# Handing out side work after every column chunk of the input projection instead of after every quarter

## Chip, cores, metric

One core of a Trainium2 chip. The metric is device microseconds of one execution; the median of three runs of the kernel before is 2044.25 us (2044.1, 2044.25 and 2047.47 us).

## What is computed

One step of a hybrid decoder layer for 1024 prompt tokens and 8 decode tokens (1032 columns of activations, 2048 wide). The parts that matter here:

```
h = rmsnorm(x, norm_w)
p = h @ w_in                      # one wide projection, 7768 columns, split into q, k, v, indexer q/k, gates, ...
att  = dsa_prompt(...)            # per 128 queries: indexer scores, top 256 keys, softmax over those keys
h_ml = mlstm_run(...)             # chunked linear attention with a state that is carried along the sequence
...                               # the same two for 8 decode tokens, from paged caches and stored states
x = x + concat([att * silu(z_att), norm(h_ml) * sigmoid(o) * silu(z_ml)]) @ w_out
y = rmsnorm(x, final_norm_w)
```

Everything is float32 in and out. The matrix products run in a reduced float32 format, and each is made of three passes: operands are split into a high and a low part, and high x high, high x low and low x high are added up in PSUM.

## The kernel before

**The projection.** `w_in` is cut into 61 tiles of 128 columns (tile 0 has 88), named by `t`; their order is that of the constants `T_MISC` to `T_AZ`. For one tile, `proj` (L1359) runs four quarters `q`. A quarter covers four of the sixteen 128-row blocks of the contraction. Its weights come by one DMA on SyncE's queue (`wraw`, L210), are cast by ScalarE (`wH`, L213), and the rest is taken by VectorE (`wL`, L214). Then `mm` (L1351 to L1357) multiplies: for each of the three column chunks `c` of 344 activations (two chunks of 388 in tiles 1 to 8), 4 blocks x 3 passes = 12 matmuls into the PSUM tile `pj` of that chunk. So a quarter is 36 matmuls on TensorE, all on line L1356. After the fourth quarter `evac` (L319) takes the three `pj` tiles out on VectorE (`ev`, L333, or L331 where a scale is applied), and sends them on by DMA; for some tiles ScalarE applies sigmoid (L380, L385, L399).

**Side work.** Attention, recurrence and the decode tokens are written as Python generators ("jobs") that issue some instructions and then `yield` the weight of what is to come. Two `Lane`s hold them in order. Lane 0: `gates`, `index` (scores L458 to L463, the search for the 256th largest score L493 to L515, the mask L526 to L535), `att` (L538 on: scores L602, transposes L644, casts `ptH`, `ptL` L648 and L649, values L653), `ml` (recurrence, L775 on: transposes and products L817 to L822, casts L787 and L829, main products L841 to L847, `tail` L877). Lane 1: `dscore` (L964), `dsel` (L1000, L1080), `datt` (decode attention: L919 to L921, `qb` loads L1216, products L1235 and L1239, values L1280), `dml` (decode recurrence: loads `bc` L1149 and `Cb` L1152, scale L1163, update L1165).

Each job has a start and an end, counted in projection tiles. `Lane.step(now)` takes 1 off the lane's debt and then runs generator steps until the debt is paid; a step costs

```
quarters = max(1.0, self.job.end * 4 - self.now)
cost = w * quarters / max(self.left, w)
```

so that the job's remaining weight is spread over the remaining quarters. `proj` calls it once behind the three chunks of each quarter:

```
for lane in lanes:
    lane.step(ts[0] * 4 + q)
```

Jobs start at tile 9 (`T_AK`) at the earliest and the last ones are to end at tile 58 (`T_PRE`). At two places the rest of a job is run at once (`ensure`): `att` ahead of tile 53, `ml` and `dml` at tile 58.

**What sets the real order.** The Python order gives priorities. A list scheduler at build time reorders the instructions of every engine from these, from the data they need and from its own plan of how long each takes; `tc.high_priority()` lifts the loads and casts of projection weights and `evac`, and `pin` keeps single instructions in program order. Each engine then runs its list in order. Side products use five PSUM banks (`bank`), the projection three (`pj`).

**Behind the projection** come two output stages: L1483 (the part of the tokens from 640 on) and L1521 (tokens 0 to 639), which no lane takes part in.

Of the kernel before, what the change touches and what calls it, by code (L numbers as in the profile page):

```python
# [41 lines left out]
T_AK = 9  # L42
# [48 lines left out]
    return c  # L91


class Job:
    def __init__(self, name, start, end, weight, gen, *conds):
        self.name, self.start, self.end, self.weight, self.gen, self.conds = name, start, end, weight, gen, conds


class Lane:
# [7 lines left out]
    def _next(self):  # L107
        if self.cur is None:
            self.job = self.jobs.pop(0)
            self.left = self.job.weight  # L110
            self.cur = self.job.gen()
        try:
            w = next(self.cur)
        except StopIteration:
            self.done.add(self.job.name)
            self.cur = None
            return 0.0
        quarters = max(1.0, self.job.end * 4 - self.now)
        cost = w * quarters / max(self.left, w)
        self.left -= w  # L120
        return cost

    def _ready(self):
        return bool(self.jobs) and self.jobs[0].start * 4 <= self.now and all(f() for f in self.jobs[0].conds)

    def step(self, now):
        self.now = now
# [13 lines left out]
def body(tc, A, stop=None):  # L141
# [58 lines left out]
    def bank(n=512, dt=F32, parts=128):  # L200
        t = psg.tile([128, 512], F32, name="bank")
        return t
# [15 lines left out]
    def wsplit(src, cols, pool, raws, bufs, tie=False, tag=""):  # L218
        H, L, load, cast = wload(src, cols, pool, raws, bufs, tag)
        dma = load(slice(0, 4))  # L220
        if tie:
            pin(dma)
        cast(slice(0, 4))
        return H, L
# [81 lines left out]
    def chunks(t):  # L306
        return CHQ if T_IQ <= t < T_AK else CH
# [1015 lines left out]
    def mixload(ci, k, pool, tie=False):  # L1323
        c0, cn = CB[ci]
        h = pool.tile([128, cn], F32R, name=f"mH{k}", bufs=1)
        l = pool.tile([128, cn], F32R, name=f"mL{k}", bufs=1)
        dma = SY.dma_start(l.bitcast(F32), gateV[k, :, c0:c0 + cn])
        if tie:
            pin(dma)
        src = attS[k // 4][(k % 4) * 128:(k % 4 + 1) * 128] if k < 8 else hS[(k - 8) * 128:(k - 7) * 128]  # L1330
        SY.dma_start(h.bitcast(F32), src[:, c0:c0 + cn])
        return ci, k, pool, h, l

    def mixmake(ci, k, pool, h, l, tie=False, tmp=None):
        c0, cn = CB[ci]
        oo, mr = h.bitcast(F32), l.bitcast(F32)
        mx = (tmp or pool).tile([128, cn], F32, name="mx", bufs=2)
        if k < 8:
            v = V.tensor_tensor(mx, mr, oo, OP.mult)
        else:  # L1340
            v = V.scalar_tensor_tensor(mx, oo, mlw[:, k - 8:k - 7], mr, OP.mult, OP.mult)
        if tie:
            pin(v)
        SC.copy(h, mx)
        V.tensor_tensor(l, mx, h.bitcast(F32), OP.subtract)
        mixb[ci][k] = (h, l)

    def wsrc(t, q):
        return A["wm"][q] if t == 0 else A["wa"][t - 1, q]

    def mm(ps, cols, t, q, c, H, L):  # L1351
        c0, cn = chunks(t)[c]
        for k in range(4):
            kk = q * 4 + k
            for w_, x_, z in ((H, xH, 0), (H, xL, 1), (L, xH, 2)):
                PE.matmul(ps[:cols, :cn], w_[:, k, :cols], x_[kk][:, c0:c0 + cn],  # L1356
                          start=(kk == 0 and z == 0), stop=(kk == 15 and z == 2))  # L1357

    def proj(ts, hook=None):  # L1359
        pss = []  # L1360
        for x, t in enumerate(ts):
            nc_ = len(chunks(t))
            if x:
                pss.append([bank() for c in range(nc_)])
            else:
                pss.append([psj.tile([128, 512], F32, name=f"pj{(t * nc_ + c) % 3}") for c in range(nc_)])
        for q in range(4):
            ws = []
            for x, t in enumerate(ts):
                cols = NMISC if t == 0 else 128  # L1370
                with tc.high_priority():
                    if hook and x == 0:
                        hook(q, ws)
                    elif hook and not q:
                        pass
                    elif x:
                        ws.append(wsplit(wsrc(t, q), cols, x0, 2, 4, q == 1))
                    else:
                        ws.append(wsplit(wsrc(t, q), cols, wst, 2, 3))
            for x, t in enumerate(ts):  # L1380
                cols = NMISC if t == 0 else 128
                H, L = ws[x]
                for c in range(len(pss[x])):
                    mm(pss[x][c], cols, t, q, c, H, L)
            for lane in lanes:
                lane.step(ts[0] * 4 + q)
            if len(mids) > 3 or mids and not pend:
                for _ in range(2):
                    mixmake(*mids.pop(0), True)
            for k in pend[:2]:  # L1390
                mids.append(mixload(0, pend.pop(0), pb0, True))
        return pss
# [4 lines left out]
    def xhook(q, ws):  # L1397
# [4 lines left out]
        for k in range(max(1, q * 4), q * 4 + 4):  # L1402
            xload(k)
            if k == 2:
                SY.dma_start(cst, A["cst"][:, :NCST])
                with tc.tile_pool(name="c0", bufs=1) as c0p:
# [3 lines left out]
                    V.tensor_copy(cmask[:, 128:256], ctmp[:, 128:256])  # L1410

    pss = proj((0, 1, 2), xhook)
    with tc.high_priority():
        for _ in row_rstd([acc], rstd, R, x0):
            pass
    x0ctx.close()
    with tc.tile_pool(name="mp", bufs=1) as mp, tc.tile_pool(name="iqp", bufs=1) as iqp:
        with tc.high_priority():
            misc = evac(0, pss[0], NMISC, mp)
        with tc.high_priority():  # L1420
            for t in (1, 2):
                evac(t, pss[t], 128, iqp)
        for t in range(3, T_AK):
            pss = proj((t,))
            with tc.high_priority():
                evac(t, pss[0], 128, iqp)
            if t == 3:
                index_weights(misc)
    for t in range(T_AK, NT):
        if t == T_AZ:  # L1430
            lanes[0].ensure("att")
        norms = load_norms(t) if t >= T_AZ else None
        pss = proj((t,))
        if t == T_PRE:
            lanes[0].ensure("ml")
            lanes[1].ensure("dml")
            pb0 = mctx.enter_context(tc.tile_pool(name="pb0", bufs=1, side="right"))
        with tc.high_priority():
            evac(t, pss[0], 128, None, norms)
        if t == T_PRE:  # L1440
            pend += PRE
# [67 lines left out]
    def resid(g):  # L1509
        for b in range(NBK):  # L1510
            yt[b][g] = pt.tile([128, 512], F32, name=f"yt{b}{g}")
            SY.dma_start(yt[b][g], A["x2"][b, :, g * 512:g * 512 + 512])
        f = pt.tile([128, 512], F32, name="fnr")
        SY.dma_start(f, A["fnr"][g * 512:g * 512 + 512].partition_broadcast(128))
        return f
# [34 lines left out]
    for g in range(4):  # L1550
        ps = [bank() if x is None else psj.tile([128, 512], F32, name=f"pj{x}") for x in homes[g]]
        ws = []
        for n in range(KT):
# [5 lines left out]
            if n == 5:  # L1559
                f = resid(g)  # L1560
# [94 lines left out]
```

## Time and profile before

| | |
|---|---|
| median of three runs | 2044.25 us |
| profiled execution | 2045.44 us, of which 2043.7 us are its span |
| outside the span | 1.74 us |
| TensorE (PE) busy | 2027.0 us, 99% of the span |
| VectorE (DVE), ScalarE (ACT), GpSimd (POOL) busy | 58%, 40%, 11% |
| mean granted TensorE clock | 0.997 |

Times are microseconds from the first instruction. PE's matmuls overlap in the records (each is shown for 0.32 us where a new one starts every 0.157 us), so a busy time counts stretches in which some matmul was under way.

### The profile page before, as it was taken

To read this page: it belongs to the slowest core of one execution; us is meant where nothing else is said; L and a number is where in the kernel's file an instruction comes from. 1 tells how busy PE (TensorE), PEld (TensorE's weight loads), DVE (VectorE), ACT (ScalarE), POOL (GpSimd) and SP (SyncE) were. 2 spreads that over 40 slices of the span, in tenths; PEclk is the share of its full clock that TensorE was granted. 3 is DMA by queue.
4 is the path that set the end of the run, shared out by engine and by line. 5 is a ranking of instruction groups with operands and counts; after the bars stand their busy time and mean duration, and the time that the engine had idled before them with its cause. 6 is when DMAs were issued, how large, how long until landed. Compare 5 with 4: busy or idle time off the path is not lost.

```text
span 2043.7 us, 34345 instructions
## 1 busy us (share of the span) xinstructions
PE 2027.0 (99%) x12678; PEld 1954.4 (96%) x12678; DVE 1178.0 (58%) x2955; ACT 820.5 (40%) x1616; POOL 233.7 (11%) x294
## 2 busy tenths in 40 slices
PE   9999999999999999999999999999999999999998
PEld 8999999999999999999999999999999999998886
DVE  8333357656686776878354554446677456664331
ACT  8121234233531455312256666544454334433221
POOL 0000111100000000023110011012222211101110
PEclk9999999999999999999999999999999999999999
DMA  7444533322222212244322332146675558566212
GB/s 246 105 112 125 155 109 114 102 81 65 79 70 75 77 49 67 68 140 155 112 74 82 111 96 85 48 130 197 210 216 174 149 183 315 176 224 223 81 49 103
DMA packets 203669, 257.08 MB, mean 126 GB/s; under 512 B 39685, under 2 KB 130885, under 8 KB 203501
## 3 DMA queue, kind: packets, MB, share of 16 engines
q1 hardware_dynamic: 198253, 240.82, 37.9%
q0 software_dynamic: 4096, 12.59, 2.0%
q8 instruction: 99, 1.62, 0.3%
q10 hardware_dynamic: 1152, 1.49, 0.2%
q14 instruction: 69, 0.57, 0.1%
HBM read 195.00 MB, written 59.82 MB: 125 GB/s over the span
## 4 chain that ended last, share of the span: by engine, by line
PE 94%; issue 2%; DVE 2%; ACT 1%; DMA 1%; SPq 0%; POOLq 0%; POOL 0%; DVEq 0%; ACTq 0%
PE pj L1356 61%; PE bank L1483 7%; PE bank L1521 6%; PE pj L1521 4%; PE bank L458 3%; PE bank L653 2%; PE bank L602 2%; PE bank L644 1%; PE bank L964 1%; PE bank L1356 1%; DMA xr<-in_xT_dram 1%; PE bank L841 1%; PE bank L847 1%; PE bank L843 1%; PE bank L1080 0%
## 5 line engine op out<-in xcount | busy, mean ns | idle before, releaser
L1356 PE MATMUL pj<-xH,wH 128*128 128x344 f32 (+2 forms) x2736 | 882.9, 324 | 3.0 <-DVE ev L333 1.5
L1356 PE MATMUL pj<-xH,wL 128*128 128x344 f32 (+2 forms) x2736 | 882.2, 323 | 0.0
L1356 PE MATMUL pj<-xL,wH 128*128 128x344 f32 (+2 forms) x2736 | 881.9, 323 | 0.0
L1356 PEld LDWEIGHTS pj<-xH,wH 128*128 128x128 f32 (+1 forms) x2736 | 513.8, 188 | 6.4 <-ACT wH L213 1.8
L1356 PEld LDWEIGHTS pj<-xL,wH 128*128 128x128 f32 (+1 forms) x2736 | 513.6, 188 | 2.9 <-DVE xL L266 0.9
L1356 PEld LDWEIGHTS pj<-xH,wL 128*128 128x128 f32 (+1 forms) x2736 | 514.1, 188 | 2.2
L213 ACT CAST wH<-wraw 128x512 fp32r<-128x512 f32 (+2 forms) x375 | 228.8, 614 | 642.4 <-PE pj L1356 413.0
L214 DVE TENSOR_TENSOR wL<-wraw,wH 128x512 fp32r<-128x512 f32 (+2 forms) x375 | 263.5, 708 | 339.7 <-ACT wH L213 325.3
L507 ACT ACTIVATE eq<-eq 128x512 bf16<-128x512 bf16 (+2 forms) x93 | 78.4, 843 | 114.1 <-DVE eq L506 111.4
L333 DVE TENSOR_TENSOR ev<-pj,rstd 128x344 f32<-128x344 f32 x144 | 74.0, 514 | 70.3 <-PE pj L1356 58.1
L460 ACT ACTIVATE rl<-bank 128x512 f32<-128x512 f32 (+2 forms) x160 | 78.7, 522 | 89.0 <-PE bank L458 63.3
L463 DVE SCALAR_TENSOR_TENSOR s<-rl,wiN,s 128x512 f32<-128x512 f32 (+2 forms) x150 | 94.8, 655 | 27.1 <-ACT rl L460 24.3
L1483 PE MATMUL bank<-mL,wH 128*128 128x392 f32 x256 | 87.2, 341 | 0.0
L1483 PE MATMUL bank<-mH,wL 128*128 128x392 f32 x256 | 86.9, 341 | 0.0
L1483 PE MATMUL bank<-mH,wH 128*128 128x392 f32 x256 | 86.2, 341 | 0.0
L649 DVE TENSOR_TENSOR ptL<-bank,ptH 128x512 fp32r<-128x512 f32 (+1 forms) x80 | 50.6, 635 | 57.3 <-ACT ptH L648 56.6
L458 PE MATMUL bank<-ki,qi 128*128 128x512 f32 (+2 forms) x320 | 76.3, 358 | 0.0
L1521 PE MATMUL bank<-wH,mH 128*128 128x512 f32 x192 | 75.4, 393 | 0.0
L1521 PE MATMUL bank<-wH,mL 128*128 128x512 f32 x192 | 75.2, 392 | 0.0
L1521 PE MATMUL bank<-wL,mH 128*128 128x512 f32 x192 | 75.2, 392 | 0.0
L336 POOL COPY dec<-ev 128x8 f32<-128x8 f32 x28 | 15.3, 545 | 514.9 <-DVE ev L333 262.4
L648 ACT CAST ptH<-bank 128x512 fp32r<-128x512 f32 (+1 forms) x80 | 42.8, 541 | 55.2 <-PE bank L644 54.0
(391 smaller groups left out, 2890.4 us busy)
## 6 DMA issues: line engine op xcount, KB each, us to landing
wraw<-in_wa_dram SPq DMA_DIRECT2D x238, 256.0 KB
wraw<-in_wo_dram SPq DMA_DIRECT2D x64, 256.0 KB
wraw<-in_wt_dram SPq DMA_DIRECT2D x64, 256.0 KB
gateS<-ev SPq DMA_DIRECT2D x72, 172.0 KB
qkv<-mlS SPq DMA_DIRECT2D x16, 512.0 KB
xr<-in_xT_dram SPq DMA_DIRECT2D x15, 516.0 KB
qi<-qS SPq DMA_DIRECT2D x24, 256.0 KB
mlS<-ev SPq DMA_DIRECT2D x48, 128.0 KB
```

The source lines that it names most:

```text
L213: a = SC.copy(H[:, s, :cols], raw[:, s, :cols])
L214: return a, V.tensor_tensor(L[:, s, :cols], raw[:, s, :cols], H[:, s, :cols].bitcast(F32), OP.subtract)
L333: V.tensor_tensor(e, ps[c][:cols, :cn], rstd[:cols, c0:c0 + cn], OP.mult)
L458: PE.matmul(p[:, :cn], qi[:, h % 4, :], ki[x][:, c0:c0 + cn], start=(x == 0), stop=(x == 1))
L460: SC.activation(r[:, :cn], p[:, :cn], AF.Relu)
L463: v = V.scalar_tensor_tensor(s[:, c0:c0 + cn], r[:, :cn], wv, s[:, c0:c0 + cn], OP.mult, OP.add)
L507: SC.activation(junk2[:, :W1], junk2[:, :W1], AF.Copy, accum_out=cnt[:, 1:2])
L648: SC.copy(pH[:, :kw], pt[:, :kw])
L649: V.tensor_tensor(pL[:, :kw], pt[:, :kw], pH[:, :kw].bitcast(F32), OP.subtract)
L1356: PE.matmul(ps[:cols, :cn], w_[:, k, :cols], x_[kk][:, c0:c0 + cn], start=(kk == 0 and z == 0), stop=(kk == 15 and z == 2))
L1483: PE.matmul(p, w_[:, k, :], x_, start=(n == 0), stop=(n == 47))
L1521: PE.matmul(p, x_[:, bs], w_.rearrange("p a b -> p (a b)"), start=(n == 0 and z == 0), stop=(n == KT - 1 and z == 2))
```

## The change

`Lane.step` is called behind every chunk: 12 matmuls instead of 36. The clock of the lanes counts twelfths of a tile instead of quarters, and the cost of a generator step is scaled with it, so a job's pace in tiles stays what it was. Tiles below 9, in which no job can start, no longer call it. The generators, their yields and weights are unchanged.

```
+STEPS = 12
...
-        quarters = max(1.0, self.job.end * 4 - self.now)
-        cost = w * quarters / max(self.left, w)
+        steps = max(1.0, self.job.end * STEPS - self.now)
+        cost = w * steps / max(self.left, w)
...
-        return bool(self.jobs) and self.jobs[0].start * 4 <= self.now and all(f() for f in self.jobs[0].conds)
+        return bool(self.jobs) and self.jobs[0].start * STEPS <= self.now and all(f() for f in self.jobs[0].conds)
...
                 for c in range(len(pss[x])):
                     mm(pss[x][c], cols, t, q, c, H, L)
-            for lane in lanes:
-                lane.step(ts[0] * 4 + q)
+                    if t >= T_AK:
+                        for lane in lanes:
+                            lane.step(t * STEPS + q * 3 + c)
```

## The prediction

> **What bounds the kernel.** I read three views first. Part 1 of the page and the group of costliest instructions say which engine fills the span:
>
> ```profile
> PE 2027.0 (99%) x12678; PEld 1954.4 (96%) x12678; DVE 1178.0 (58%) x2955; ACT 820.5 (40%) x1616; POOL 233.7 (11%) x294
> ...
> PE 94%; issue 2%; DVE 2%; ACT 1%; DMA 1%; SPq 0%; POOLq 0%; POOL 0%; DVEq 0%; ACTq 0%
> ```
>
> The second line is the chain that ended last: 94% of it is matmul time. But a share over the whole span hides stages, so I cut the span where the jobs change. The columns of this view are window, its length, busy time (and instructions) of PE, PEld, DVE, ACT, POOL, the granted clock, DMA share and GB/s:
>
> ```profile
> 188.00:560.00 372.00, 372.00 (x2433) 366.60 (x2432) 221.10 (x592) 133.91 (x310) 39.15 (x46) 1.00 0.33 102
> 560.00:880.00 320.00, 320.00 (x2180) 308.82 (x2179) 245.16 (x666) 129.99 (x241) 5.07 (x12) 1.00 0.24 69
> 880.00:1010.00 130.00, 128.48 (x809) 126.52 (x808) 82.03 (x133) 25.65 (x43) 40.85 (x40) 0.97 0.47 150
> 1010.00:1300.00 290.00, 287.45 (x1965) 281.64 (x1965) 146.26 (x484) 175.87 (x373) 22.15 (x24) 1.00 0.28 84
> 1300.00:1613.00 313.00, 313.00 (x2107) 310.14 (x2105) 195.32 (x637) 150.13 (x309) 64.05 (x114) 1.00 0.53 166
> 970.00:980.00 10.00, 10.00 (x52) 10.00 (x52) 1.21 (x1) 0.62 (x1) 7.05 (x8) 0.66 0.38 116
> ```
>
> These five stretches, 188 to 1613, are all in which lanes hand out work. PE is idle in them for 130.00 - 128.48 = 1.52 us in the decode attention and 290.00 - 287.45 = 2.55 us in the prompt attention, and not at all in the other three: 4.07 us together. Who ended those waits (PE's waits between 215 and 1613; total, times, longest):
>
> ```profile
> PE bank L653 <- ACT ptH L648: 2.1, 2, 1.6
> PE pj L1356 <- DVE ev L333: 1.5, 1, 1.5
> PE bank L644 <- ACT pP L618: 0.5, 1, 0.5
> ```
>
> Four waits. "Busy" could still hide matmuls that start late, so I looked at the rate, in the chain of waits:
>
> ```profile
> 960.31 5.98 PE pj L1356 x38
> ...
> 970.93 2.95 PE bank L1280 x24
> 973.88 6.30 PE pj L1356 x22
> ...
> 1365.26 5.66 PE pj L1356 x36
> ```
>
> A quarter in the recurrence stage takes 5.66/36 = 0.157 us a matmul, one in the decode stage 5.98/38 = 0.157. The 22 behind the L1280 burst take 0.286: that is the half clock which the 0.66 of window 970 to 980 shows, and it costs 10 x (1 - 0.66) = 3.4 us. So all that a different hand-out could give back is 4.07 us of waits and 3.4 us of slow clock, 7.5 us or 0.37%.
>
> **The change, part by part.** About 0.2% (4.1 us) is what a measurement of this kernel can tell from no change.
>
> *Matmuls.* No generator step is added, dropped or altered, so each engine gets the same compute instructions and PE streams the same columns. Cost 0.
>
> *Placement.* On paper a hand-out now follows 12 x 0.157 = 1.9 us of projection instead of 5.7. But the built order is the scheduler's. In the two built programs I counted the runs of side matmuls that stand between projection matmuls: 324 before and 344 after. Before was already finely mixed. I also took, for every PE instruction that waits for ACT or DVE, the matmul time that stands between the product which feeds it and itself, with each shape's start-to-start time from this trace. For transposes to values (L644 by L648 to L653) the smallest is 3.2 us before and 3.0 after, the middle 3.8 in both; for an emptied `pj` the smallest is 24 x 0.157 = 3.8 in both, which occurs 35 times before and 24 after; for weights 6.7 in both; for the recurrence (L819 by L787 to L843) 6.1 in both. Distances of 3.2 and 3.8 cost no wait in this trace except at the four places above. Cost 0, and I find no new tight place for PE.
>
> *Prompt attention, -1.5 us.* The waits for L648 come when ScalarE changes its function table:
>
> ```profile
> 1118.79 1.28 ACT L618 ACT_TABLE_LOAD   x1
> 1120.08 0.72 ACT L618 ACTIVATE pP<-pP,st 128x512 f32<-128x512 f32 x1
> 1120.71 0.19 ACT L618 ACTIVATION_READ_ACCUMULATOR pP<-pP,st 128x1 f32 x1
> 1120.92 1.28 ACT L385 ACT_TABLE_LOAD   x1
> ...
> 1122.86 0.59 ACT L648 CAST ptH<-bank 128x512 fp32r<-128x512 f32 x1
> ...
> 1123.50 0.39 PE L653 MATMUL bank<-ptH,vH 128*128 128x256 f32 x1 [1.64 <-ACT ptH L648]
> ```
>
> Exp for attention and sigmoid for the gates alternate, two loads of 1.28 us stand ahead of the cast, and PE waits 1.64.
>
> ```profile
> L618 ACT ACT_TABLE_LOAD x18 | 23.1, 1283 | 2.2 <-DVE st L615 1.9
> L385 ACT ACT_TABLE_LOAD x13 | 16.7, 1283 | 10.1 <-DVE ev L333 9.5 <-issue 0.5
> L380 ACT ACT_TABLE_LOAD x11 | 14.1, 1283 | 0.2
> L809 ACT ACT_TABLE_LOAD x9 | 11.5, 1283 | 0.2
> ```
>
> In the changed program L618 has 12 such loads, L385 10, L380 10 and L809 11; 54 in all instead of 62, so ScalarE has 8 x 1.283 = 10.3 us less to do, though it still alternates. That time is hidden beside PE except in those waits: gain between 0 and 2.55 us. I take 1.5, nearer the upper end since the line that stands in the largest wait, L618, loses a third of its loads.
>
> *Decode attention, -0.6 us.* DVE waits for the first `qb` and its queue piles up ahead of `ev`:
>
> ```profile
> 887.73 1.22 DVE L528 TENSOR_REDUCE sm<-gt 128x1 f32<-128x1024 bf16 x1
> 888.86 2.28 DVE L531 TENSOR_TENSOR_SCAN s<-eq 128x1024 f32<-128x1024 bf16 x1
> ...
> 892.13 1.28 DVE L532 SCALAR_TENSOR_TENSOR eq<-s,sm,eq 128x1024 bf16<-128x1024 f32 x1
> ...
> 894.35 0.51 DVE L333 TENSOR_TENSOR ev<-pj,rstd 128x344 f32<-128x344 f32 x1
> 894.77 0.42 DVE L534 TENSOR_SCALAR gt<-gt 128x1024 bf16<-128x1024 bf16 x1
> ...
> 896.69 0.44 SPq L535 DMA_DIRECT2D biasS<-gt  x1
> ...
> 908.29 1.23 DVE L1235 TENSOR_TENSOR jk<-kv,qb 128x1024 f32<-128x1024 f32 x1 [5.03 <-DMA qb<-qrowS]
> 909.43 0.68 DVE L214 TENSOR_TENSOR wL<-wraw,wH 128x512 fp32r<-128x512 f32 x1
> 910.03 1.21 DVE L1239 TENSOR_REDUCE lT<-jk 128x8 f32<-128x1024 f32 x1
> ...
> 916.66 0.51 DVE L333 TENSOR_TENSOR ev<-pj,rstd 128x344 f32<-128x344 f32 x1
> ```
>
> `ev` ends at 917.17 and PE had wanted it 1.5 us before. In the changed order DVE empties the three `pj` ahead of the last mask steps, not between them. These steps take 1.22 + 2.28 + 1.28 us and small ones like L534's 0.42, about 6 us in all, and follow the third `ev` (894.35 before), so L534 ends some 5 us later, near 900. SyncE's queue, through which L535, L921 and L1216 go, held L535 back by 1.5 us before and would be free by then, so `qb` lands some 3.5 us later, near 911.8. But only L1235, L1239, L214 and L1235 stand ahead of `ev` then, instead of eight: 1.23 + 1.21 + 0.68 + 1.23 = 4.4 us. `ev` ends near 916.7, and PE waits 0.9 to 1.1 instead of 1.5. Bounds: 0 if it clears, about 3 if `qb` slips a further 2 us. Change -0.6, between -1.5 and +1.5.
>
> *Decode recurrence, +1.0 us.* The `Cb` load of the next step is issued closer to its use: the matmul time between the last event that frees its issue and the scale L1163 is 8.7 us at the least before, 1.7 at one place after and 6 to 7.5 at five others. It lands in
>
> ```profile
> 1500.43 0.33 SPq L1152 DMA_DIRECT2D Cb<-in_sC_dram  x1
> ...
> 1504.38 0.91 ACT L1163 ACTIVATE Cb<-Cb,w 128x256 f32<-128x256 f32 x2 [2.30 <-DMA Cb<-in_sC_dram]
> ```
>
> 3.9 us, and ScalarE waits in order; behind it stand the recurrence's casts (L829, L787), for which L843 on PE waits. That 2.30 us wait cost PE nothing (no idle in 1300 to 1613), which is the lower bound; the upper is the one clearly short place, 3.9 - 1.7 = 2.2 us. I take 1.0.
>
> Sum on the profiled execution: 2045.44 + 0 - 1.5 - 0.6 + 1.0 = 2044.3. That execution was 1.2 us above the median of the three runs, so the forecast for a median is 2044.25 - 1.1 = **2043.2 us**.
>
> **The clock, weighed.** In the trace 24 products of four columns in 2.95 us were followed by half clock, though PE counts as busy all through. [...]
>
> **Rivals.**
>
> *The dip goes (0.13).* [...]
>
> *A second dip (0.16).* [...]
>
> *`Cb` late at several places (0.13).* If SyncE's queue holds loads back by 3 us as well, the five places with 6 to 7.5 us turn into ScalarE waits of up to 1 us, the first one into 5; were all passed to PE, 10 us: 2053. More likely a third: 2047. Against: ScalarE is 48% busy there, and the wait seen cost nothing.
>
> *The change doesn't do what it says (0.08).* The scheduler mixes so well that waits stay where they are: 2044.25.
>
> **Numbers.** The forecast as summed has 0.50. Of the dip that goes, 0.08 is over 0.2% faster (below 2040.2) and 0.05 within. Of the second dip 0.08 and of late `Cb` 0.08 are over 0.2% slower (above 2048.3). The forecast and the last rival stay within, except 0.02 for more waits than I found. Together: faster 0.08, same 0.74, slower 0.18. The range from 2039.5 to 2049.0 holds the forecast, its bounds from 2044.25 - 1.5 - 2.55 = 2040.2 to 2044.25 + 1.5 + 2.2 = 2048.0, the lost dip and one added dip; it leaves out two dips and a `Cb` late everywhere.
>
> **What would show it.** Windows cut at the same jobs: PE idle of 1 us or so in decode attention, under 2 in prompt attention, none elsewhere. ACT_TABLE_LOAD on L618 12 times. A clock below 1.00 in the window of L1280, once. Right for the wrong reason: the same time with waits at L843. Wrong: PE idle over 5 us between 188 and 1613, or a pace of the 36 matmuls other than 5.66 us at full clock.

## The result: 10 us slower

| kernel | median, us | ratio to before (95%) | profiled execution: own time, span |
|---|---|---|---|
| before | 2044.17 (2043.73 to 2047.47, 6 runs) | | 2045.44, 2043.7 |
| changed | 2053.97 (2050.52 to 2054.99, 6 runs) | 1.004 [1.003, 1.005] | 2053.93, 2052.1 |

A ratio is estimated from all the runs of a line, so it can differ a little from the quotient of two medians. Lines of the changed kernel stand 3 further down than before (L1356 is now L1359, L1163 is L1166, L843 is L846).

The same five stretches as before, with the same columns:

```profile
188.00:560.00 372.00, 370.82 (x2424) 364.86 (x2424) 228.61 (x624) 137.64 (x318) 35.34 (x43) 1.00 0.33 102
560.00:880.00 320.00, 320.00 (x2178) 308.84 (x2177) 233.09 (x626) 124.69 (x229) 6.08 (x12) 1.00 0.23 67
880.00:1010.00 130.00, 126.32 (x800) 124.67 (x798) 83.86 (x129) 26.40 (x42) 39.42 (x40) 0.97 0.49 151
1010.00:1300.00 290.00, 290.00 (x1982) 284.98 (x1981) 150.33 (x497) 163.83 (x365) 23.61 (x24) 1.00 0.28 85
1300.00:1613.00 313.00, 308.50 (x2052) 303.60 (x2051) 192.54 (x631) 148.80 (x306) 61.30 (x111) 0.99 0.53 162
```

PE's idle time by stage is now 1.18, 0, 3.68, 0 and 4.50 us, where it was 0, 0, 1.52, 2.55 and 0. The prompt attention's waits are gone; the recurrence stage, which had none, has the most. PE's waits between 188 and 1613 (total, times, longest):

```profile
PE bank L846 <- ACT dH L790: 3.6, 1, 3.6
PE pj L1359 <- DVE ev L336: 2.2, 1, 2.2
PE bank L1283 <- DMA kv<-in_cv_dram,idxs: 1.5, 1, 1.5
PE bank L461 <- DMA qi<-qS: 1.2, 1, 1.2
PE bank L846 <- DVE dL L791: 0.7, 3, 0.3
```

A wait on ScalarE's cast `dH` is the largest:

```profile
1510.51 0.55 PE L846 MATMUL bank<-aH,dH 128*128 128x258 f32 x1 [3.62 <-ACT dH L790]
```

ScalarE's own timeline around it (start, duration, and in brackets its idle time before and what ended it):

```profile
1490.14 0.91 ACT L1166 ACTIVATE Cb<-Cb,w 128x256 f32<-128x256 f32 x2
1492.91 0.90 ACT L1166 ACTIVATE Cb<-Cb,w 128x256 f32<-128x256 f32 x2
...
1499.13 0.62 ACT L216 CAST wH<-wraw 128x512 fp32r<-128x512 f32 x1
1508.68 0.91 ACT L1166 ACTIVATE Cb<-Cb,w 128x256 f32<-128x256 f32 x2 [8.94 <-DMA Cb<-in_sC_dram]
...
1509.96 0.40 ACT L790 CAST dH<-d 128x256 fp32r<-128x256 f32 x1
```

The cast did not wait for its data, which VectorE had ready at 1502.29: it stood behind the scale of `Cb`, and that waited 8.94 us for its load. Two decode steps had been put 2.8 us apart (1490.14 and 1492.91), and a third came due at 1499.7. SyncE's queue shows what became of their loads (start, duration):

```profile
1494.04 1.16 SPq L1173 DMA_DIRECT2D out_C_s_dram<-Cb  x2
...
1497.11 1.65 SPq L1152 DMA_DIRECT2D bc<-krowS  x2
1500.81 0.33 SPq L1155 DMA_DIRECT2D Cb<-in_sC_dram  x1
1501.24 0.86 SPq L1152 DMA_DIRECT2D bc<-krowS  x2
1502.14 0.42 SPq L1155 DMA_DIRECT2D Cb<-in_sC_dram  x1
```

Both stores are issued from 1494.04 on, both loads only at 1500.81 and 1502.14. The trace's landing records say why: the second store lands at 1500.75, and SyncE, in order, issues the first load 0.06 us later and the second behind it. It is the second that the scale at 1508.68 wants; the first lands at 1503.54, for a scale at 1517.06. So the two loads stand on the queue in the reverse of the order in which they are used. From the chain of waits, the second load's way to PE (start, length, what):

```profile
1502.14 6.43 DMA Cb<-in_sC_dram
1508.68 0.52 ACT Cb L1166
...
1515.14 2.65 PE pj L1359 x12
```

The 6.43 us are its landing. That is long but not new: by the landing records the sixteen `Cb` loads of before took 3.5 to 6.3 us, those of the changed kernel 2.7 to 6.8. And the 12 projection matmuls after it take 2.65/12 = 0.22 us each instead of 0.157: for the first part of them PE was at half clock (granted clock 0.50 from 1509.84 to 1516.67). Windows around the places where the clock fell:

```profile
919.00:923.00 4.00, 4.00 (x18) 4.00 (x17) 4.00 (x6) 0.00 (x0) 1.30 (x3) 0.57 0.92 269
980.00:984.00 4.00, 4.00 (x19) 4.00 (x20) 0.69 (x1) 0.62 (x1) 2.87 (x4) 0.60 0.34 102
1509.00:1517.00 8.00, 6.33 (x23) 5.63 (x24) 5.60 (x19) 4.04 (x12) 0.41 (x2) 0.57 0.42 134
```

The losses at half clock are 4 x 0.43 = 1.7, 4 x 0.40 = 1.6 and 8 x 0.43 = 3.4 us. The granted-clock record has these stretches as 3.4, 3.4 and 6.8 us long, half of which is 6.8 us lost in all, against 3.4 before. So the span can be added up: PE's idle time grew by 9.36 - 4.07 = 5.3 us and the time lost to the clock by 3.4, together 8.7; the span grew by 2052.1 - 2043.7 = 8.4. Of the 8.7, the recurrence has 4.50 + 3.4 = 7.9, the decode attention 2.16, the index stage 1.18, and the prompt attention gives 2.55 back. The sum is rough in two ways: some idle time lies inside the half-clock stretch, and since the records overlap (at 925 us in the changed kernel each is 0.32 us long and the next starts 0.16 us after it), a short gap looks shorter than it is.

### The profile page after: what moved, and what is told of

Its sections match the earlier page's. It is cut to its first block, busy times and chain, and to the rows that moved or that the text cites. A ratio compares the mean times of both kernels' runs of the same rounds, so it can differ in the third digit from the quotient of the medians.

```text
span 2052.1 us, 34329 instructions
## 1 busy us (share of the span) xinstructions
PE 2029.2 (99%) x12678; PEld 1954.3 (95%) x12678; DVE 1181.3 (58%) x2955; ACT 809.0 (39%) x1608; POOL 235.2 (11%) x294
## 3 DMA queue, kind: packets, MB, share of 16 engines
q10 hardware_dynamic: 1152, 1.49, 0.2%
## 5 line engine op out<-in xcount | busy, mean ns | idle before, releaser
L1359 PE MATMUL pj<-xH,wH 128*128 128x344 f32 (+2 forms) x2736 | 885.0, 325 | 4.2 <-DVE ev L336 2.2
L1359 PE MATMUL pj<-xL,wH 128*128 128x344 f32 (+2 forms) x2736 | 882.0, 323 | 0.2 <-DVE xL L269 0.2
L1359 PE MATMUL pj<-xH,wL 128*128 128x344 f32 (+2 forms) x2736 | 882.2, 323 | 0.0
L1359 PEld LDWEIGHTS pj<-xH,wH 128*128 128x128 f32 (+1 forms) x2736 | 514.3, 188 | 8.5 <-ACT xH L268 2.8
L1359 PEld LDWEIGHTS pj<-xL,wH 128*128 128x128 f32 (+1 forms) x2736 | 513.9, 188 | 3.3 <-DVE xL L269 1.0
L1359 PEld LDWEIGHTS pj<-xH,wL 128*128 128x128 f32 (+1 forms) x2736 | 514.1, 188 | 1.9
L461 PE MATMUL bank<-ki,qi 128*128 128x512 f32 (+2 forms) x320 | 78.0, 358 | 1.2 <-DMA qi<-qS 1.2
```

The lines of the kernel that those rows point to most:

```text
L461: PE.matmul(p[:, :cn], qi[:, h % 4, :], ki[x][:, c0:c0 + cn], start=(x == 0), stop=(x == 1))
```

## Experiments

**The theory:** the loss is the late `Cb` load of the decode recurrence: ScalarE, in order, stops for it, PE for ScalarE's casts, and the clock falls behind that. **The rival:** the finer hand-out costs a little in every stage, and the wait for `Cb` is hidden as it was before.

In all kernels by chunk or quarter, one helper is used: the lanes count twelfths, and a quarter's hand-out takes three of them off the debt at once.

```
-lane.step(t * STEPS + q * 3 + c)
+if CONDITION:  lane.step(t * STEPS + q * 3 + c)
+elif c == 2:   lane.step(t * STEPS + q * 3, 3.0)      # as before the change
```

Lines of these kernels stand 5 further down than before (L848 is L843). That the helper itself moves nothing is seen in `e5_chunk_att` below, whose order is that of before on every engine. The kernel before was run again beside each group of experiments, with medians of 2044.07, 2044.47 and 2044.58 us; the ratios below are to these runs.

### Where: the last ten tiles

`e1_quarter_late`: CONDITION is `t < 48`.

> The changed kernel, but from projection tile 48 on (recurrence of prompt and decode tokens) side work is handed out once a quarter again. Theory A (the loss is the decode recurrence's state loads, which come too late, stop ScalarE and through it TensorE, and bring a half-clock stretch): 2054.0 less 4.5 us of idle TensorE and 3.4 us of clock, about 2046; PE idle in 1300 to 1613 under 0.5 us. Theory B (the loss is spread over all stages in proportion to their length): 313 of 1425 us undone, about 2052.

`e2_chunk_late`: CONDITION is `t >= 48`.

> The kernel before, but from tile 48 on handed out after every chunk. Theory A: 2044.2 + 7.9, about 2052, with a wait of ScalarE for the state load Cb of over 5 us. Theory B: 2044.2 + 22% of 9.8, about 2046, without such a wait.

Measured: `e1_quarter_late` 2043.98 us, ratio 0.9996 [0.9987, 1.0005]; `e2_chunk_late` 2050.68, ratio 1.0032 [1.002, 1.0044]. The window 1300 to 1613 of the first and then of the second, and the second's waits of ScalarE for `Cb` and of PE:

```profile
1300.00:1613.00 313.00, 313.00 (x2108) 310.02 (x2108) 193.61 (x637) 146.69 (x306) 63.77 (x114) 1.00 0.55 166
```

```profile
1300.00:1613.00 313.00, 309.05 (x2069) 304.43 (x2068) 196.67 (x635) 153.28 (x311) 62.80 (x113) 1.00 0.54 163
...
ACT Cb L1168 <- DMA Cb<-in_sC_dram: 10.2, 3, 7.7
...
PE bank L848 <- ACT dH L792: 3.2, 2, 2.4
```

Theory A had 2046 and 2052. Without the late tiles the loss is gone; with them alone 6 of the 10 us are there, and they come with a wait for `Cb` of 7.7 us and PE idle behind `dH`. The rival, by which these tiles would carry 22% of the loss, falls.

The orders on PE let this be counted exactly. In the traces `e1_quarter_late` has the changed kernel's order, and `e2_chunk_late` that of before, up to the 8839th matmul (near 1360 us). From there to the projection's last matmul before and `e1_quarter_late` take 314.0 us, `e2_chunk_late` 319.4 and the changed kernel 322.8: a growth of 5.4 and of 8.8 us. The 2052 us expected of `e2_chunk_late` held 3.4 us of clock. In its profiled execution that part is missing: the clock record has no half-clock stretch in this stage. Its longest gap on PE is shorter, too:

```profile
1510.29 0.36 PE L848 MATMUL bank<-aH,dH 128*128 128x258 f32 x1 [2.38 <-ACT dH L792]
```

ScalarE's wait less the gap on PE behind it is the same in both kernels with the loss: 8.94 - 3.62 = 5.3 and 7.70 - 2.38 = 5.3 us. At this place ScalarE could stand for 5.3 us before PE did, and the 1.24 us by which the two waits differ are 1.24 us more of gap.

### What: the load of Cb

`e3_after_deep` is the changed kernel, `e4_before_deep` the kernel before, both with a third `Cb` buffer and the load placed two steps ahead in the program:

```
-Cb = pc.tile([128, 2, 2, 128], F32, name="Cb")
+Cb = pc.tile([128, 2, 2, 128], F32, name="Cb", bufs=3)
...
+Cs = [fetchC(0, 0), fetchC(0, 1)]
...
+if b + 1 < NB: Cs.append(fetchC(b + 1, u))
```

> The changed kernel, with a third buffer for the decode state Cb and its load issued two steps ahead, so that it does not wait for the store of the step before. Theory A: ScalarE's wait for Cb falls under 1 us, 2046. Theory B: 2053 to 2054. A third way (theory C: the wait moves to the other load, bc, or to the store): 2050 to 2054 with DVE waiting for bc.

> The kernel before with the same third buffer and earlier load. Theories A and B: its one wait for Cb cost TensorE nothing, so 2044.2 within 1 us. If merely another order of instructions moves the time by several us (theory D), it may lie 2 us or more off.

Measured: 2043.85 us, ratio 1.0 [0.9991, 1.0009], and 2045.15, ratio 1.0003 [0.9994, 1.0012]. The waits for `Cb` in that stage, of `e3_after_deep` and of `e4_before_deep`:

```profile
ACT Cb L1172 <- DMA Cb<-in_sC_dram: 5.2, 2, 3.1
```

```profile
ACT Cb L1169 <- DMA Cb<-in_sC_dram: 4.6, 1, 4.6
```

With this edit the changed kernel loses its long wait and the 10 us together, and the kernel before stays within 0.1% of its time. The wait did not fall under 1 us, as theory A had it: 3.1 us were left. They cost next to nothing (PE was idle 0.14 us in the stage), and the 4.6 us of `e4_before_deep` cost nothing (PE busy 313.00 of 313.00 us), which fits the 5.3 us above. The scheduler moved some scales in answer to this edit too, so these two runs alone do not part the load from the order; the next one looks at that.

### Why the load was late

`e11_after_buf3` has the third buffer only (`bufs=3`); the loads are issued at the same places of the program.

> The changed kernel with a third Cb buffer and nothing else: each load is issued at the same place in the program, but goes into a buffer that was stored one step earlier. If the load comes late because it waits until the store of the step just done has landed: ScalarE's longest wait for Cb shrinks from 8.9 us to 5 or less, PE has no wait on L846's counterpart in 1300 to 1613, 2044 to 2046. If it comes late because it stands behind the other stores and loads in SyncE's queue, or because three steps lie within 16 us: the wait stays at 7 to 9 us, 2050 to 2054.

Measured: median 2046.07, ratio 1.0001 [0.9992, 1.001]. ScalarE's waits for `Cb` and the window of the stage:

```profile
1300.00:1613.00 313.00, 312.96 (x2109) 309.64 (x2108) 196.70 (x640) 152.09 (x313) 64.41 (x114) 1.00 0.54 163
...
ACT Cb L1166 <- DMA Cb<-in_sC_dram: 6.4, 2, 3.7
```

The wait is 3.7 us at most, PE's idle time in the stage 0.04, as the first expectation has it; but its reason is not what the trace shows. SyncE still issues two loads right behind the landing of a store (landing records: store issued at 1496.95, landed at 1501.39; loads issued at 1501.45 and 1502.79), no earlier than without the buffer. What differs is which load is wanted:

```profile
1494.57 0.89 ACT L1166 ACTIVATE Cb<-Cb,w 128x256 f32<-128x256 f32 x2
1504.33 0.91 ACT L1166 ACTIVATE Cb<-Cb,w 128x256 f32<-128x256 f32 x2 [2.73 <-DMA Cb<-in_sC_dram]
```

The scale that is due waits for the first of the two loads, which lands at 1504.30, 2.85 us after its issue; the second lands at 1508.40, when nothing waits for it yet. On ScalarE the traces differ from the changed kernel's in the place of three pairs of scales and one cast: the step ahead of the one at 1494.57 now stands 12.4 us earlier (1482.20), where the two were 2.8 us apart. `e3_after_deep` has the same order on PE and ScalarE and differs on SyncE in a few places only, so moving the load in the program, on top of the buffer, changed little. How much of the cure is the buffer and how much the order was not separated; shown is that the load wanted stood second behind a store's landing with the loss, and first without it. Had it stood first in the changed kernel, it would by estimate have landed at 1503.54, 3.8 us after the scale came due at 1499.74, which is within the 5.3.

Its eleven runs lie in two groups, 2042.3 to 2044.1 (five) and 2046.1 to 2047.3 (six). The profiled execution is of the upper one (span 2045.5), and its clock record has three half-clock stretches of 3.4 us in the decode attention, where before had 6.8 us in one. That fits the groups' distance, but no profile of the lower group was taken.

### Which lane

`e6_lane0`: CONDITION is "lane 0"; `e7_lane1`: "lane 1".

> Lane 0 (prompt's index, attention, recurrence) by chunk, lane 1 (decode) by quarter. If it is the decode lane's own finer hand-out that sets two of its steps close together: no wait for Cb over 5 us, no PE idle in 1300 to 1613, prompt attention without its waits, 2041 to 2042.5. If it is the prompt recurrence's finer hand-out that moves the scheduler's order under the decode steps: one wait for Cb near 9 us, a half-clock stretch near 1510, 2050 to 2052.

> Lane 1 (decode) by chunk, lane 0 by quarter: the counterpart. If the decode lane's own hand-out is the cause: one wait of ScalarE for Cb of 7 to 9 us, PE idle of 3 to 4.5 us in 1300 to 1613, the prompt attention's two waits on L653 as before, 2050 to 2054. If lane 0's is: no such wait, 2044 to 2046.

Measured: 2044.6 us, ratio 1.0005 [0.9995, 1.0014], and 2043.09, ratio 0.9992 [0.9983, 1.0001]. Neither has the long wait; the longest for a `Cb` load is 2.3 us in the first and 2.9 in the second. Both expectations of a single guilty lane missed: the long wait comes only where both lanes are handed out by chunk. Steps close together are not enough for it. `e7_lane1` has two of them 1.9 us apart, and a third 8.5 us behind:

```profile
1499.65 0.91 ACT L1168 ACTIVATE Cb<-Cb,w 128x256 f32<-128x256 f32 x2 [2.91 <-DMA Cb<-in_sC_dram]
1501.54 0.91 ACT L1168 ACTIVATE Cb<-Cb,w 128x256 f32<-128x256 f32 x2 [0.47 <-DVE hm L874]
```

Its two loads, issued at 1495.85 and 1497.18, landed at 1499.62 and 1501.43, in the order of their use. `e6_lane0` loses 4.04 us in the stage at another place (1340 to 1344), with VectorE's `ev`:

```profile
PE pj L1361 <- DVE ev L338: 4.0, 2, 2.2
```

Why the scheduler reverses the two loads only with both lanes was not settled.

### The prompt attention's gain

`e5_chunk_att`: CONDITION is `40 <= t < 48`, where the prompt attention's waits were. `e8_att_deep`: the same with the deep `Cb` load.

> Chunk hand-out only for tiles 40 to 47, where the prompt attention's waits went; quarters everywhere else. Late-load theory (the loss lies in the decode recurrence alone, the gain in the prompt attention is kept): no wait on L841 to L850 between 1300 and 1613, PE idle 0 there and 0 in 1010 to 1300, decode attention as before; 2044.4 - 3.6 = 2041, and 2044 at the most if the half-clock stretch of the gathers falls longer. Spread theory (each stage loses or gains a little by the finer hand-out, the table loads have nothing to do with it): 2044 to 2045, with the waits on L653 still there.

> Chunk hand-out for tiles 40 to 47 alone, and the third Cb buffer with its load two steps ahead. Late-load theory: the recurrence has nothing to lose any more and had no idle before, so the same as the first of these, 2041, within 1 us of it. If the waits for Cb of 2 to 5 us that cost PE no idle time nevertheless slow it by what stands behind them: 1 to 2 us less than the first, 2039 to 2040.

Measured: 2043.9 us, ratio 1.0 [0.9991, 1.0009], and 2044.33, ratio 1.0002 [0.9993, 1.0011]. The late-load theory's expectation of 2041 missed, and the first one's waits say why:

```profile
PE bank L658 <- ACT ptH L653: 2.1, 2, 1.6
PE pj L1361 <- DVE ev L338: 1.4, 1, 1.4
PE bank L649 <- ACT pP L623: 0.5, 1, 0.5
```

These are the waits of before. In the traces the order of `e5_chunk_att` is that of before, instruction by instruction on all five engines: in these eight tiles the scheduler makes the same order of both hand-outs. `e1_quarter_late`, by chunk up to tile 47, has none of the waits, so the hand-out before tile 40 was needed to move them; the work then arrives in another order.

### A version that beats both

`e9_lane1_early`: CONDITION is "lane 1 and `t < 48`"; `e10_lane0_early`: "lane 0 and `t < 48`".

> The decode lane by chunk up to tile 47, all else by quarter; the recurrence stage is built as before. From the run with the decode lane by chunk throughout: 0.57 us of PE idle in the decode attention, none in the prompt attention, and none in the recurrence, so 3.5 us less idle than before: 2040.5, by which it would beat both kernels. If PE's idle time is not what the median follows (that run had 2.6 us less idle and was 1.0 us faster): 2042 to 2044.

> The prompt lane by chunk up to tile 47, all else by quarter. From the run with the prompt lane by chunk throughout: 0.55 us idle in the index stage, 0.14 in the decode attention, 0.87 in the prompt attention, none in the recurrence: 2.5 us less idle than before, 2041.5. If idle time is not what the median follows: 2043 to 2044.5.

Measured: 2040.5 us, ratio 0.9981 [0.9972, 0.999], and 2044.51, ratio 1.0002 [0.9993, 1.0011]. The first beats both kernels, by 0.19% against the one before, at the time expected. That is about the least that the prediction said could be told from no change; the interval leaves out 1, but it is one build. Its stages from the decode attention on, and all of PE's waits between 188 and 1613:

```profile
880.00:1010.00 130.00, 129.35 (x827) 126.65 (x826) 76.84 (x146) 35.78 (x61) 38.84 (x40) 0.99 0.49 151
1010.00:1300.00 290.00, 290.00 (x1995) 285.44 (x1994) 148.63 (x491) 169.65 (x373) 23.46 (x24) 1.00 0.27 83
1300.00:1613.00 313.00, 313.00 (x2098) 310.94 (x2097) 186.23 (x605) 141.62 (x287) 63.68 (x114) 1.00 0.54 166
...
PE bank L570 <- DMA qL<-aqS: 0.5, 1, 0.5
```

0.65 us of idle time are left of 4.07, and one half-clock stretch of 3.4 us (1.7 us lost) instead of 6.8. From before's span: 2043.7 - 3.4 - 1.7 = 2038.6, measured 2038.3. With one order the idle time stayed and the clock's part did not: `e5_chunk_att`, in the order of before on every engine, has 3.96 us of idle time for 4.07, but 1.7 us lost at half clock for 3.4. `e10_lane0_early` did not reach 2041.5: VectorE's `ev` is late twice at the head of its recurrence stage, 3.8 us, at the same place as in `e6_lane0`.

The same sum, 2043.7 plus the growth of the idle time between 188 and 1613 plus that of the time lost at half clock, against the span of every profile:

| kernel | idle, us | lost at half clock, us | sum | span |
|---|---|---|---|---|
| changed | 9.36 | 6.8 | 2052.4 | 2052.1 |
| `e1_quarter_late` | 3.14 | 3.4 | 2042.8 | 2042.3 |
| `e2_chunk_late` | 8.61 | 1.7 | 2046.5 | 2050.1 |
| `e3_after_deep` | 3.68 | 1.7 | 2041.6 | 2041.2 |
| `e4_before_deep` | 4.52 | 1.7 | 2042.5 | 2043.4 |
| `e5_chunk_att` | 3.96 | 1.7 | 2041.9 | 2041.7 |
| `e6_lane0` | 5.60 | 1.7 | 2043.5 | 2042.8 |
| `e7_lane1` | 1.49 | 1.7 | 2039.4 | 2042.1 |
| `e8_att_deep` | 3.94 | 1.7 | 2041.9 | 2041.8 |
| `e9_lane1_early` | 0.65 | 1.7 | 2038.6 | 2038.3 |
| `e10_lane0_early` | 4.68 | 1.7 | 2042.6 | 2042.4 |
| `e11_after_buf3` | 3.92 | 5.1 | 2045.2 | 2045.5 |

Ten of twelve agree within 0.9 us. That is partly luck, since the sum leaves out what comes ahead of the side work. The first 1119 matmuls stand in one order in all thirteen traces, and the next one starts at 198.1 us in before, at 197.1 in the changed kernel and at 200.2 in `e7_lane1`. That is 2.1 of the 2.7 us missing for `e7_lane1`. Of the 3.6 missing for `e2_chunk_late`, 1.2 arise there too (199.3), and 1.4 are the growth of 5.4 us by the count of matmuls less the 3.95 that show as idle; 1.0 is left unexplained.

## Why the prediction was wrong

**The forecast** of 2043.2 and its range to 2049.0 missed 2053.97. Its own sign of being wrong, more than 5 us of PE idle between 188 and 1613, came: 9.36. The likeliest case had no large loss, and the step that failed is "Decode recurrence, +1.0 us".

**The step that failed.** Its mechanism was right: a `Cb` load issued close to its use, ScalarE in order, PE behind it. Its size was not: +1.0, at most 2.2, against 7.9 measured in the stage by idle time and clock, and 8.8 by the count of matmuls. Three terms were short. (1) The issue, the largest. The step had the load issued 1.7 us ahead of its use at the shortest place. If that is the place of the loss, it was issued 2.4 us after the scale came due (1502.14 against 1499.74), 4.1 us worse: it stood on SyncE's queue behind another load, and that behind the landing of a store (issued at 1494.86, landed at 1500.75, by the landing records). (2) The landing: 3.9 us was one row, where before's sixteen loads took up to 6.3; it was 6.43 us, 2.5 worse. The 2.2 of the prediction with 4.1 and 2.5 are 8.8 of the 8.94 us that ScalarE waited. (3) The consequence: the step passed ScalarE's wait to PE one to one, from 0 up. The runs show a slack of 5.3 us first, so its 2.2 would have cost nothing; and with a gap of 3.6 us in PE, up to 1510.51, came 6.8 us of half clock, from 1509.84 on: 3.4 us more, which the step did not count.

**The rival that named it**, "`Cb` late at several places", had 0.13 and gave 2047 to 2053. The upper end is nearly the time measured, though it was one place, late by 8.9 us, and not five late by 1.

**Prompt attention, -1.5 us:** -2.55 measured, the upper bound. Table loads fell as counted; ScalarE's work in the stage went from 175.87 to 163.83 us. The stage has 31 table loads before, 21 in the changed kernel, and 24 and 25 in `e9_lane1_early` and `e10_lane0_early`, whose idle time there is 0 and 0.86 us: fewer loads go with, rather than prove, the waits' end. The cause was not in these tiles alone (`e5_chunk_att`), and the step gave no reason by which all of the 2.55 would go, so the size was in part luck.

**Decode attention, -0.6 us:** +2.16 measured, outside its bounds of -1.5 and +1.5. The steps held for a while (VectorE of the changed kernel):

```profile
900.87 0.43 DVE L537 TENSOR_SCALAR gt<-gt 128x1024 bf16<-128x1024 bf16 x1
...
913.73 1.23 DVE L1238 TENSOR_TENSOR jk<-kv,qb 128x1024 f32<-128x1024 f32 x1 [4.48 <-DMA qb<-qrowS]
...
917.86 0.51 DVE L336 TENSOR_TENSOR ev<-pj,rstd 128x344 f32<-128x344 f32 x1
```

The mask ended at 901.3 (near 900 forecast), and the instructions ahead of `ev` were the four forecast. But the first `qb` load was issued 6.0 us later than before (909.47 for 903.48) and VectorE started at 913.7, 1.9 us later than the 911.8 reckoned, so `ev` ended at 918.4 and not 916.7, and PE waited 2.2 instead of about 1. That is 0.7 of the 2.16; the rest is the gathers. The gathers' wait of 1.5 us (L1283) and the index stage's of 1.2 (L461) were not foreseen at all.

**The clock.** No run shows what makes the clock fall: the chances of 0.13 and 0.16 for a dip less and a second dip, and their place in the range at 3.4 us each, the loss in before, were the author's estimate. The runs showed 3.4 us lost at half clock between 188 and 1613 before, 6.8 in the changed kernel, and 1.7 in `e5_chunk_att` with the order of before. The half clock in the decode attention stayed at 6.8 us, in two parts, one of them from 919.34 on, behind 2.2 us of idle PE that ended at 918.51; the added 6.8 us began at 1509.84, in the gap of 3.6 us. **Placement, 0 us:** the search covered distances on PE to ScalarE and VectorE. It could not find the new waits: the four largest have a load from memory behind them, of `Cb`, `qb`, `kv` and `qi`.

## What to carry to other kernels

Where a list scheduler decides the order, a finer hand-out is no finer interleaving: in one stage it moved nothing, in another it put two steps of a double-buffered loop together and their next loads in the wrong order. Before such a change, look for the in-order engine that both the loop and the critical engine need (here ScalarE, which stood for 8.94 us), and see where its loads stand behind its own stores. To judge a change below half a per cent, add up idle time by stage and time at reduced clock, and try its parts by stage and by lane: the part that pays may lie elsewhere than the part that was meant to.

## What the hardware showed

In the clock records of before and of the changed kernel each half-clock stretch in the lanes' stages was 3.4 or 6.8 us long, at a granted clock of 0.50: one of 6.83 us before, and 3.41, 3.41 and 6.83 in the changed kernel. The other eleven profiles lost 1.7, 3.4 or 5.1 us there (table above). In both records all changes of the clock lie on one grid of 3.413 us: in the changed kernel the stretches start at 919.34, 980.78 and 1509.84, so the second and third come 61.44 and 590.50 us after the first, which is 18 and 173 steps. The length of a gap alone does not decide: PE's wait for `ev` in the decode attention was 2.2 us in the changed kernel, and a stretch began 0.8 us after its end; none came with the gap of 2.4 us at 1510 in `e2_chunk_late` (clock 1.00 from 1505 to 1520). Kernels with the same order up to tile 48 had 6.8 us of half clock in the decode attention (before, clock 0.97), none (`e2_chunk_late`, 1.00) and 3.4 (`e4_before_deep`, 0.99). Over the executions of the kernel before that ran beside the experiments the mean granted clock was 0.996 to 0.999. These runs put the price of one stretch of 3.4 us at 1.7 us, which is as much as most of the waits looked for here.

One row is no measure of a landing. In the recurrence stage the sixteen `Cb` loads of before, 256 KB each, landed 3.5 to 6.3 us after their issue, and those of the changed kernel 2.7 to 6.8. The sixteen stores of the same size took 2.0 to 4.5 us before and 2.0 to 6.1 in the changed kernel. The longest two there were issued 0.8 us apart, but two stores 1.3 us apart in before (1506.14 and 1507.45) took 2.0 us each: what made the difference was not tested.
